# Attention's turns one unit later, late modulation sums one request later, in a one-core diffusion layer

## The chip, the core and the metric

The kernel runs on one core of one Trainium2 chip. What is measured is the device time of one execution in microseconds (us), lower is better. Each row of a profile comes from one execution that was recorded by the hardware profiler; its times are microseconds from the start of the span unless marked ns. The engines are TensorE (PE, with its weight loads as PEld), VectorE (DVE), ScalarE (ACT), GpSimd (POOL) and SyncE (SP, which here only issues DMAs).

## What is computed

One layer over 256 latent tokens and 256 context tokens, width 2048, all float32. Cut to its steps:

```
mod = silu(c) @ w_mod + b_mod                  # sa, ca, ga, sm, cm, gm: six vectors of 2048
h   = rmsnorm(x) * (1 + ca) + sa               # the same for the context tokens, with c_ctx
q, k, v, pool_in, gates = h @ w_in             # context gives k and v only
p   = softmax(q k^T / 8) per head half;  a = p0 - lam * p1;  heads = a @ v     # 8 heads
y_a = (rmsnorm(heads) * 0.8) @ w_a_up;  y_b = multiscale_pool(pool_in) @ w_b_up
x   = x + ga * ((g_a * y_a + g_b * y_b) @ w_o)     # g = sigmoid(gates)
x   = x + gm * (relu(modulate(x, sm, cm) @ w_ff1)^2 @ w_ff2)      # w_ff1: 2048 x 8192
```

`sa` and `ca` are needed at once. `ga`, `cm`, `sm` and `gm` are needed only from the product with `w_o` on; the kernel calls them late modulation.

## The kernel before, in words

**Weights.** All weights stream from HBM once, as chunks of 128 x 1024 floats (512 KB) in the order of a list `stream`. `load_next` issues one chunk's DMA on SP into one of five buffers `raw`, then splits it into two float32r parts: ACT casts `whi` (L195 before), DVE subtracts `wlo` (L196). A chunk's product takes three matmuls for each pair of slices (hi*hi, hi*lo, lo*hi). `whi` and `wlo` have three buffers each, so the split runs two chunks ahead of the matmuls. `wchunk` hands out the next chunk and calls `tick`.

**Late modulation.** `late_gen` is a generator with one step for each 128 x 1024 chunk of `w_ga`, `w_cm`, `w_sm`, `w_gm` (32 chunks each, two halves of 16). `load_next` adds a stage's rate to a credit and takes one step per whole credit: 1.0 for the first value group and the second query group, 1.5 for the second key and value groups, 0.75 in the pooling, 0.42 in the gates, 0.25 in the product with `w_o` (0 in its last group) and after. A step issues the chunk's DMA into the same five `raw` buffers and adds the chunk to an accumulator `macc` on DVE (L533). After 16 steps a half is split (`ah`, `al`) and summed over partitions by two matmuls with ones (`late_sum`).

**Deferred work.** `later(n, fn)` puts a function on a list; each `wchunk` ticks the list and runs what is due, so that `n` counts chunks. `flush` runs the whole list. Turning the normed queries and keys (`qkT`), the norm of a pair of heads (`osum`), the pooling's difference and the turning of the gated mixture (`mixT`) are put there.

**Attention** runs beside the bulk products. `run(bulk, side, EVERY)` advances the generator `attention` once for every 4.4 tokens' worth of bulk chunks. A unit is one head and one block of 128 queries: `scores` does two score matmuls (`sc`), then DVE takes the maxima (`mx`), ACT exponentiates (`e`), DVE combines the two halves into `e` (L602). `a_transpose` turns `e` on PE (`aTp`), `av` multiplies with the values (`ob`).

**The end of the product with `w_o`.** For its last group, g = 3, DVE and ACT instructions are held in program order (`ordered`): the residual, its squares, the rsqrt (`rsq`), then `flush()`, then the shift `yt` by `sm` (`shifted(0)`), whose turned result (`h2T`, `hidden2(0)`) the first MLP product waits for. Before it, a loop steps `late_gen` until `gm` has begun:

```
        if g == 3:
            while "gm" not in mods:
                next(late[0])
        ordered[0] = g == 3
```

**The order of instructions** on each engine is fixed when the program is built: a scheduler lists them by its own forecast of when each will be ready, except where `pin` (`keep_in_program_order`) holds an instruction in the order of the code. At run time every engine takes its list strictly in order.

Of the kernel before, what the change touches and what calls it, by code (L numbers as in the profile page):

```python
# [48 lines left out]
def layer(ctx: ExitStack, tc, a, out):  # L49
# [20 lines left out]
        return psum.tile([P, 512], F32, tag="ps", name=name)  # L70

    def work(name, shape=None, dt=F32):
        return pool.tile(shape or [P, 512], dt, tag="w2", name=name, bufs=7)

    def s16(name, shape, dt=F32):
        return pool.tile(shape, dt, tag="s16", name=name, bufs=7)
# [9 lines left out]

    late = [None]
    credit = [0.0]

    waiting = []  # L90

# [83 lines left out]
    def load_next():  # L175
        key, rate = stream[len(loaded)]
        src = a[key[0]]
        for i in key[1:]:
            src = src[i]
        if key[0] in ("cT", "x"):  # L180
            dst = cT[:, 4 * key[1]:4 * key[1] + 4, :] if key[0] == "cT" else x1_tile()[:, key[1], key[2] * 512:key[2] * 512 + 512]
            nc.sync.dma_start(dst, src)
            loaded.append((key, None, None))
            return
        n = src.shape[-1]
        raw = raw_chunk(src, n)
        if key[:2] in (("w_k", 0), ("w_q", 0)) and key[2] < 7:
            if not first:
                first.append(s16("first", [P, 4, 1024], F32R))
            i = 0 if key[0] == "w_k" else 2  # L190
            hi, lo = first[0][:, i, :], first[0][:, i + 1, :]
        else:
            hi = pool.tile([P, n], F32R, tag="whi", name="whi", bufs=3)
            lo = pool.tile([P, n], F32R, tag="wlo", name="wlo", bufs=3)
        act.copy(hi, raw)  # L195
        vec.tensor_sub(lo, raw, hi.bitcast(F32))  # L196
        loaded.append((key, hi, lo))
        credit[0] += rate
        while credit[0] >= 1.0:
            credit[0] -= 1.0  # L200
            if late[0] is not None:
                next(late[0], None)
# [309 lines left out]

    ga_bc = s8("ga_bc", [P, D])
    mods = {}

    def late_gen():
        for name in ("ga", "cm", "sm", "gm"):
            if name == "ga":
                dst = ga_bc
            elif name == "gm":  # L520
                mods["gm"] = s8("gm_bc", [P, D])
                dst = mods["gm"]
            else:
                if "sb" not in mods:
                    mods["sb"] = s16("sb", [P, 2, D])
                dst = mods["sb"][:, 0 if name == "cm" else 1, :]
            for half in range(2):
                acc = pool.tile([P, 1024], F32, tag="macc", name="macc", bufs=2)
                gp.memset(acc, 0.0)
                nc.gpsimd.dma_start(acc[0:1, :], a["b_" + name][half])  # L530
                for k in range(KT):
                    raw = raw_chunk(a["w_" + name][half, k])
                    vec.scalar_tensor_tensor(acc, raw, sil[:, 0, k:k + 1], acc, ALU.mult, ALU.add)  # L533
                    yield
                for q in range(2):
                    ah, al = work("ah", dt=F32R), work("al", dt=F32R)
                    split(ah, al, acc[:, q * 512:q * 512 + 512])
                    later(4 + q, partial(late_sum, name, ah, al, 2 * half + q,
                                         dst[:, half * 1024 + q * 512:half * 1024 + q * 512 + 512]))

    def late_sum(name, ah, al, i, o):

        ps = bank("late")
        pin(pe.matmul(ps, ones, ah, start=True, stop=False))
        pe.matmul(ps, ones, al, start=False, stop=True)
        if name == "cm":
            wr = work("nmw")
            nc.gpsimd.dma_start(wr, a["nmw"][i])
            vec.scalar_tensor_tensor(o, ps, 1.0, wr, ALU.add, ALU.mult)
        else:  # L550
            act.copy(o, ps)
# [14 lines left out]
    def k_group(g):  # L566
        bs = [bank(f"k{g}_{t}") for t in range(4)]
        yield from xstat(("w_k", g), bs, tokens(4))
        for t in range(4):
            qk_evac(bs[t], t, g, kT, 2, 2 + t)  # L570

    def q_group(g):
        bs = [bank(f"q{g}_{t}") for t in range(2)]
        for _ in xstat(("w_q", g), bs, tokens(2)):
            yield 0
        for t in range(2):
            qk_evac(bs[t], t, g, qT, 0, 3 + t)

    oT = pairtile("oT")
    heads = [0]  # L580
# [32 lines left out]
    def av(h):  # L613
# [7 lines left out]
        if h % 2 == 1:  # L621
# [14 lines left out]
                split(oT[:, 0, h - 1:h + 1, :], oT[:, 1, h - 1:h + 1, :], o2)  # L636
                heads[0] += 2

            later(3, norm)

    def attention(h0, h1):
        units = [(h, qt) for h in range(h0, h1) for qt in range(2)]
        prev = None
        for u in units + [None]:
            while u and turned[u[0] // 4] < 6 or prev and prev[0][1] == 1 and values[0] < prev[0][0]:
                yield
            cur = scores(*u) if u else None
            if prev is not None:
                (h, qt), at = prev
                a_transpose(h, qt, at)  # L650
                if qt == 1 and h > h0:
                    av(h - 1)
            if u is None:
                yield
                av(h1 - 1)
            prev = (u, cur)
            yield


    ybh = [None]  # L660
# [2 lines left out]
    def pooling():  # L663
# [3 lines left out]
        for g, w in enumerate(WINDOWS):  # L667
# [12 lines left out]
            for i in range(2):  # L680
# [8 lines left out]
                    src, oth = oth, src  # L689
                    step *= 2  # L690
                sums.append(src[:, s0:s0 + T])
            later(2, partial(pool_diff, g, w, ps, sums))
            if g > 0:
                pool_out(g - 1)

# [82 lines left out]

    run(v_group(0), iter(()), 1)
    run(chain(q_group(1), k_group(1), v_group(1), pooling(), gates()), attention(0, 8), EVERY)  # L780
    flush()
    tc.keep_in_program_order(act.preload_act_table_set("natural_log_exp_and_others"))


# [253 lines left out]
```

## Time and profile before

| what | before |
|---|---|
| median of 3 runs | 1548.26 us (1546.31 to 1548.51) |
| the profiled execution | 1548.65 us, of it 1546.8 us span |
| granted TensorE clock, mean | 0.989 of 2.4 GHz |
| busy share of the span: PE, DVE, ACT, POOL | 96%, 68%, 49%, 8% |
| moved by DMA | 347.83 MB, mean 225 GB/s |

The span is the time from the first instruction to the last. The difference of 1.85 us lies around it. PE is called busy while a matmul is in flight, also when it runs at half clock, so the busy share hides the half-clock stretches; the granted clock of a stretch tells them.

### The profile page before, as it was taken

What the parts mean: (1) busy time and instruction counts of PE and PEld (TensorE: products, weight loads), DVE (VectorE), ACT (ScalarE), POOL (GpSimd) and SP (SyncE); (2) the same over time, 40 slices, a digit from 0 to 9 for tenths busy, and PEclk for the clock granted to TensorE, in tenths of its full rate; (3) what the DMA queues carried; (4) which work ended last, traced back from release to release, by engine and by line L of the source; (5) the groups of instructions that cost most, each with busy time, mean ns of one, the idle gap of its engine ahead of it and who ended that gap; (6) DMA issues with size and microseconds to landing.
All of it is one profiled execution on the core that took longest, in us unless ns stands there. A gap on an engine that the chain in (4) does not pass through costs nothing.

```text
span 1546.8 us, 19707 instructions
## 1 busy us (share of the span) xinstructions
PE 1489.0 (96%) x7304; PEld 1236.5 (80%) x7304; DVE 1057.8 (68%) x1291; ACT 755.4 (49%) x1005; POOL 124.6 (8%) x124
## 2 busy tenths in 40 slices
PE   6999998899989999999998999999999999999998
PEld 4777776667778887887888988888888888888886
DVE  6998968677777676676677665666666555555575
ACT  7777533456544443443444554544445354444532
POOL 2000101010150000000000110000000000000170
PEclk9999999999999999999999999999999999999999
DMA  9888667543558877889675677777777666666563
GB/s 342 308 296 309 214 209 266 177 137 103 164 178 282 273 252 240 270 276 319 222 223 167 204 259 239 237 231 244 223 250 222 187 192 189 194 187 194 182 197 138
DMA packets 97440, 347.83 MB, mean 225 GB/s; under 512 B 11072, under 2 KB 11712, under 8 KB 97344
## 3 DMA queue, kind: packets, MB, share of 16 engines
q1 hardware_dynamic: 96624, 345.17, 69.1%
q8 instruction: 57, 0.93, 0.3%
q0 software_dynamic: 576, 1.08, 0.2%
q10 hardware_dynamic: 144, 0.33, 0.1%
q14 instruction: 39, 0.32, 0.1%
HBM read 344.44 MB, written 2.10 MB: 224 GB/s over the span
## 4 chain that ended last, share of the span: by engine, by line
PE 78%; DMA 9%; DVE 8%; issue 2%; ACT 2%; POOL 1%; DVEq 0%; ACTq 0%; POOLq 0%; SPq 0%
PE f L887 13%; PE f L387 8%; PE f L386 8%; PE f L389 7%; PE f L890 7%; PE pg L389 3%; PE pg L387 3%; PE pg L386 3%; DVE wlo L196 3%; DMA raw<-in_w_sm_dram 3%; DMA raw<-in_w_ga_dram 2%; DMA raw<-in_w_cm_dram 2%; PE mod L322 2%; PE wo L387 2%; PE wo L386 2%
## 5 line engine op out<-in xcount | busy, mean ns | idle before, releaser
L195 ACT CAST whi<-raw 128x1024 fp32r<-128x1024 f32 x501 | 523.4, 1047 | 581.4 <-PE f L387 177.0
L196 DVE TENSOR_TENSOR wlo<-raw,whi 128x1024 fp32r<-128x1024 f32 x501 | 614.6, 1239 | 260.4 <-ACT whi L195 249.6
L533 DVE SCALAR_TENSOR_TENSOR macc<-raw,sil,macc 128x1024 f32<-128x1024 f32 x128 | 166.4, 1300 | 146.2 <-DMA raw<-in_w_sm_dram 63.0
L887 PE MATMUL f<-h,whi 128*128 128x512 f32 x896 | 224.2, 392 | 0.0
L387 PE MATMUL f<-whi,act 128*128 128x512 f32 x512 | 199.3, 389 | 0.0
L386 PE MATMUL f<-whi,act 128*128 128x512 f32 x512 | 199.3, 389 | 0.0
L887 PEld LDWEIGHTS f<-h,whi 128*128 128x128 f32 x896 | 161.5, 189 | 29.1
L389 PE MATMUL f<-wlo,act 128*128 128x512 f32 x512 | 136.8, 389 | 0.0
L890 PEld LDWEIGHTS f<-h,wlo 128*128 128x128 f32 x896 | 122.2, 190 | 8.7
L890 PE MATMUL f<-h,wlo 128*128 128x256 f32 x896 | 124.9, 282 | 0.0
L389 PEld LDWEIGHTS f<-wlo,act 128*128 128x128 f32 x512 | 96.1, 188 | 20.0
L386 PEld LDWEIGHTS f<-whi,act 128*128 128x128 f32 x512 | 96.1, 188 | 19.8
L387 PEld LDWEIGHTS f<-whi,act 128*128 128x128 f32 x512 | 96.1, 188 | 19.8
L386 PE MATMUL pg<-whi,hL 128*128 128x512 f32 x256 | 100.9, 394 | 0.0
L387 PE MATMUL pg<-whi,hL 128*128 128x512 f32 x256 | 100.6, 393 | 0.0
L389 PE MATMUL pg<-wlo,hL 128*128 128x512 f32 x256 | 69.9, 395 | 7.7 <-DVE wlo L196 7.7
L898 POOL TENSOR_TENSOR rsq<-relu 128x512 f32<-128x512 f32 x28 | 29.2, 1042 | 546.1 <-ACT relu L897 536.0
L389 PEld LDWEIGHTS pg<-wlo,hL 128*128 128x128 f32 x256 | 48.3, 190 | 19.4 <-DVE wlo L196 9.6
L387 PEld LDWEIGHTS pg<-whi,hL 128*128 128x128 f32 x256 | 48.6, 190 | 10.2
L386 PEld LDWEIGHTS pg<-whi,hL 128*128 128x128 f32 x256 | 48.6, 190 | 10.2
L386 PE MATMUL wo<-whi,mix 128*128 128x512 f32 x128 | 50.5, 394 | 0.0
L387 PE MATMUL wo<-whi,mix 128*128 128x512 f32 x128 | 50.3, 393 | 0.0
(282 smaller groups left out, 2223.5 us busy)
## 6 DMA issues: line engine op xcount, KB each, us to landing
raw<-in_w_ff_dram SPq DMA_DIRECT2D x240, 512.0 KB, 4.1
raw<-in_w_m_dram SPq DMA_DIRECT2D x64, 512.0 KB, 5.1
raw<-in_w_ga_dram SPq DMA_DIRECT2D x32, 512.0 KB, 4.4
raw<-in_w_cm_dram SPq DMA_DIRECT2D x32, 512.0 KB, 4.3
raw<-in_w_gb_in_dram SPq DMA_DIRECT2D x32, 512.0 KB, 4.9
raw<-in_w_ga_in_dram SPq DMA_DIRECT2D x32, 512.0 KB, 4.6
raw<-in_w_sm_dram SPq DMA_DIRECT2D x32, 512.0 KB, 4.6
raw<-in_w_o_dram SPq DMA_DIRECT2D x32, 512.0 KB, 4.2
```

The lines of the kernel that those rows point to most:

```text
L195: act.copy(hi, raw)
L196: vec.tensor_sub(lo, raw, hi.bitcast(F32))
L322: pe.matmul(ps, cv[:, k, :], part[:, kk * 512:kk * 512 + 512], start=(k == 0 and part is hi), stop=(k == 15 and part is lo))
L386: pe.matmul(banks[t], tok(h, k, 0, tt), wt, start=k == 0, stop=False)
L387: pe.matmul(banks[t], tok(h, k, 1, tt), wt, start=False, stop=False)
L389: pe.matmul(banks[t], tok(h, k, 0, tt), wt, start=False, stop=k == 2 * nk - 1)
L533: vec.scalar_tensor_tensor(acc, raw, sil[:, 0, k:k + 1], acc, ALU.mult, ALU.add)
L887: pe.matmul(ps, hi[:, kk * P:kk * P + P], both(h2, k), start=k == 0, stop=False)
L890: pe.matmul(ps[:, T:2 * T], lo[:, kk * P:kk * P + P], act_slice(h2, k, 0), start=False, stop=k == KT - 1)
L898: gp.tensor_mul(sq, r, r)
```

## The change

It does five things. Attention keeps two units in flight: a unit's probabilities are turned after the scores of the second unit behind it. Turns of queries and keys, the pooling's difference and the heads' norm are due one or two chunks later. A late modulation chunk is added to `macc` by a function on the list, one tick (rate 1 or more) or two ticks (rate below 1) after its request, in program order on DVE; the accumulator has one buffer instead of two, and each half of 16 begins with an empty step. The `nmw` rows that `cm` is multiplied with are loaded at the half's ninth chunk, not in `late_sum`. The work buffers go from 7 to 9, and the `flush()` between the gates and the product with `w_o` is gone. The amount of arithmetic and of loaded bytes stays the same.

```diff
@@ -70,7 +70,7 @@
         return psum.tile([P, 512], F32, tag="ps", name=name)
 
     def work(name, shape=None, dt=F32):
-        return pool.tile(shape or [P, 512], dt, tag="w2", name=name, bufs=7)
+        return pool.tile(shape or [P, 512], dt, tag="w2", name=name, bufs=9)
 
     def s16(name, shape, dt=F32):
         return pool.tile(shape, dt, tag="s16", name=name, bufs=7)
@@ -86,6 +86,7 @@
 
     late = [None]
     credit = [0.0]
+    credit_rate = [0.0]
 
     waiting = []
 
@@ -196,6 +197,7 @@
         vec.tensor_sub(lo, raw, hi.bitcast(F32))
         loaded.append((key, hi, lo))
         credit[0] += rate
+        credit_rate[0] = rate
         while credit[0] >= 1.0:
             credit[0] -= 1.0
             if late[0] is not None:
@@ -512,6 +514,7 @@
 
     ga_bc = s8("ga_bc", [P, D])
     mods = {}
+    parts = []
 
     def late_gen():
         for name in ("ga", "cm", "sm", "gm"):
@@ -525,27 +528,45 @@
                     mods["sb"] = s16("sb", [P, 2, D])
                 dst = mods["sb"][:, 0 if name == "cm" else 1, :]
             for half in range(2):
-                acc = pool.tile([P, 1024], F32, tag="macc", name="macc", bufs=2)
+                yield
+                for part in parts:
+                    if part in waiting:
+                        waiting.remove(part)
+                        part[1]()
+                acc = pool.tile([P, 1024], F32, tag="macc", name="macc", bufs=1)
                 gp.memset(acc, 0.0)
                 nc.gpsimd.dma_start(acc[0:1, :], a["b_" + name][half])
+                norm_w = []
                 for k in range(KT):
                     raw = raw_chunk(a["w_" + name][half, k])
-                    vec.scalar_tensor_tensor(acc, raw, sil[:, 0, k:k + 1], acc, ALU.mult, ALU.add)
+                    if name == "cm" and k == 8:
+                        for q in range(2):
+                            norm_w.append(work("nmw"))
+                            nc.gpsimd.dma_start(norm_w[q], a["nmw"][2 * half + q])
+                    later(2 if credit_rate[0] < 1 else 1, partial(late_part, acc, raw, k))
+                    parts.append(waiting[-1])
+                    if k == KT - 1:
+                        o = dst[:, half * 1024:half * 1024 + 1024]
+                        later(2 if credit_rate[0] < 1 else 1, partial(late_split, acc, norm_w, o))
+                        parts.append(waiting[-1])
                     yield
-                for q in range(2):
-                    ah, al = work("ah", dt=F32R), work("al", dt=F32R)
-                    split(ah, al, acc[:, q * 512:q * 512 + 512])
-                    later(4 + q, partial(late_sum, name, ah, al, 2 * half + q,
-                                         dst[:, half * 1024 + q * 512:half * 1024 + q * 512 + 512]))
-
-    def late_sum(name, ah, al, i, o):
+
+    def late_part(acc, raw, k):
+
+        pin(vec.scalar_tensor_tensor(acc, raw, sil[:, 0, k:k + 1], acc, ALU.mult, ALU.add))
+
+    def late_split(acc, norm_w, o):
+        for q in range(2):
+            ah, al = work("ah", dt=F32R), work("al", dt=F32R)
+            split(ah, al, acc[:, q * 512:q * 512 + 512])
+            later(4 + q, partial(late_sum, ah, al, norm_w[q] if norm_w else None, o[:, q * 512:q * 512 + 512]))
+
+    def late_sum(ah, al, wr, o):
 
         ps = bank("late")
         pin(pe.matmul(ps, ones, ah, start=True, stop=False))
         pe.matmul(ps, ones, al, start=False, stop=True)
-        if name == "cm":
-            wr = work("nmw")
-            nc.gpsimd.dma_start(wr, a["nmw"][i])
+        if wr is not None:
             vec.scalar_tensor_tensor(o, ps, 1.0, wr, ALU.add, ALU.mult)
         else:
             act.copy(o, ps)
@@ -567,14 +588,14 @@
         bs = [bank(f"k{g}_{t}") for t in range(4)]
         yield from xstat(("w_k", g), bs, tokens(4))
         for t in range(4):
-            qk_evac(bs[t], t, g, kT, 2, 2 + t)
+            qk_evac(bs[t], t, g, kT, 2, 3 + t)
 
     def q_group(g):
         bs = [bank(f"q{g}_{t}") for t in range(2)]
         for _ in xstat(("w_q", g), bs, tokens(2)):
             yield 0
         for t in range(2):
-            qk_evac(bs[t], t, g, qT, 0, 3 + t)
+            qk_evac(bs[t], t, g, qT, 0, 4 + t)
 
     oT = pairtile("oT")
     heads = [0]
@@ -636,25 +657,24 @@
                 split(oT[:, 0, h - 1:h + 1, :], oT[:, 1, h - 1:h + 1, :], o2)
                 heads[0] += 2
 
-            later(3, norm)
+            later(5, norm)
 
     def attention(h0, h1):
         units = [(h, qt) for h in range(h0, h1) for qt in range(2)]
-        prev = None
-        for u in units + [None]:
-            while u and turned[u[0] // 4] < 6 or prev and prev[0][1] == 1 and values[0] < prev[0][0]:
+        behind = []
+        for u in units + [None, None]:
+            while u and turned[u[0] // 4] < 6 or len(behind) == 2 and behind[0][1] == 1 and values[0] < behind[0][0]:
                 yield
-            cur = scores(*u) if u else None
-            if prev is not None:
-                (h, qt), at = prev
+            if u:
+                behind.append((*u, scores(*u)))
+            if len(behind) > 2 or not u:
+                h, qt, at = behind.pop(0)
                 a_transpose(h, qt, at)
                 if qt == 1 and h > h0:
                     av(h - 1)
-            if u is None:
-                yield
-                av(h1 - 1)
-            prev = (u, cur)
             yield
+        av(h1 - 1)
+        yield
 
 
     ybh = [None]
@@ -689,7 +709,7 @@
                     src, oth = oth, src
                     step *= 2
                 sums.append(src[:, s0:s0 + T])
-            later(2, partial(pool_diff, g, w, ps, sums))
+            later(3, partial(pool_diff, g, w, ps, sums))
             if g > 0:
                 pool_out(g - 1)
 
@@ -778,7 +798,6 @@
 
     run(v_group(0), iter(()), 1)
     run(chain(q_group(1), k_group(1), v_group(1), pooling(), gates()), attention(0, 8), EVERY)
-    flush()
     tc.keep_in_program_order(act.preload_act_table_set("natural_log_exp_and_others"))
 
 
```

Three places show how this moves instructions. Numbers behind a tile's name rise with the order of the code.

On PE, in the second key group, between products of that group: `sc` are a unit's two score matmuls, `aTp` the turning of a unit's `e`. Before:

```order
L590 MATMUL sc_2289<-kT_1444,qT_1443 128x512
L590 MATMUL sc_2292<-kT_1444,qT_1443 128x512
L610 MATMUL aTp_2306<-prm_61,e_2232 128x128 x4
...
L590 MATMUL sc_2347<-kT_1444,qT_1443 128x512
L590 MATMUL sc_2350<-kT_1444,qT_1443 128x512
L610 MATMUL aTp_2363<-prm_61,e_2296 128x128 x4
```

After:

```order
L611 MATMUL sc_2334<-kT_1444,qT_1443 128x512
L611 MATMUL sc_2337<-kT_1444,qT_1443 128x512
L631 MATMUL aTp_2351<-prm_61,e_2216 128x128 x4
...
L611 MATMUL sc_2395<-kT_1444,qT_1443 128x512
L611 MATMUL sc_2398<-kT_1444,qT_1443 128x512
L631 MATMUL aTp_2411<-prm_61,e_2280 128x128 x4
```

`e_2296` of before belongs to the scores 2289 and 2292 and is turned behind the next unit's scores, with one chunk of 24 matmuls (left out) between. `e_2216` of after belongs to scores 2209 and 2212; the scores 2273, 2276 and 2334, 2337 and two chunks of 24 matmuls stand between it and its turning.

On DVE, in the gates, while `w_sm` is summed. `raw_` numbers are the order in which SP asks for the chunks; `macc` adds a late chunk, `wlo` splits a weight chunk. Before:

```order
L196 TENSOR_TENSOR wlo_4851<-raw_4848,whi_4850 128x1024
L533 SCALAR_TENSOR_TENSOR macc_4739<-raw_4893,sil_82,macc_4739 128x1024
L196 TENSOR_TENSOR wlo_4872<-raw_4869,whi_4871 128x1024
L196 TENSOR_TENSOR wlo_4890<-raw_4887,whi_4889 128x1024
L533 SCALAR_TENSOR_TENSOR macc_4739<-raw_4950,sil_82,macc_4739 128x1024
L196 TENSOR_TENSOR wlo_4911<-raw_4908,whi_4910 128x1024
```

After:

```order
L197 TENSOR_TENSOR wlo_5061<-raw_5058,whi_5060 128x1024
L556 SCALAR_TENSOR_TENSOR macc_4969<-raw_5044,sil_82,macc_4969 128x1024
L197 TENSOR_TENSOR wlo_5080<-raw_5077,whi_5079 128x1024
L197 TENSOR_TENSOR wlo_5100<-raw_5097,whi_5099 128x1024
L221 TENSOR_TENSOR mix0_3959<-mixT_5103,mix0_3959 128x512
L221 TENSOR_TENSOR mix0_3959<-mixT_5110,mix0_3959 128x512
L556 SCALAR_TENSOR_TENSOR macc_4969<-raw_5083,sil_82,macc_4969 128x1024
```

Before, `raw_4893` is added ahead of the splits of 4869 and 4887, which were asked for earlier. After, `raw_5044` is added behind the split of 5058, which was asked for later.

On DVE, from the rsqrt at the end of the product with `w_o` to the first MLP product; `rq_y` is the rsqrt, `yt` by L65 are the first shifts (`shifted(0)`), `al` splits a finished `macc`. Before:

```order
L65 SCALAR_TENSOR_TENSOR rq_y<-rq_t,rq_y 128x2
L65 SCALAR_TENSOR_TENSOR yt<-yt,rq_y,sb 128x256 x2
L822 SCALAR_TENSOR_TENSOR yt<-yt,rq_y,sb 128x256 x3
L65 TENSOR_TENSOR h_0_6766<-h2T,h_0_6766 128x512
L65 SCALAR_TENSOR_TENSOR yt<-yt,rq_y,sb 128x256 x2
```

After, from the row behind `rq_y` on:

```order
L65 SCALAR_TENSOR_TENSOR macc<-raw,sil,macc 128x1024
L841 SCALAR_TENSOR_TENSOR yt<-yt,rq_y,sb 128x256
L65 SCALAR_TENSOR_TENSOR macc<-raw,sil,macc 128x1024
L841 SCALAR_TENSOR_TENSOR yt<-yt,rq_y,sb 128x256
L65 SCALAR_TENSOR_TENSOR macc<-raw,sil,macc 128x1024
L841 SCALAR_TENSOR_TENSOR yt<-yt,rq_y,sb 128x256
L65 SCALAR_TENSOR_TENSOR macc<-raw,sil,macc 128x1024
L841 SCALAR_TENSOR_TENSOR yt<-yt,rq_y,sb 128x256
L65 SCALAR_TENSOR_TENSOR macc<-raw,sil,macc 128x1024 x2
L65 TENSOR_TENSOR al<-macc,ah 128x512 x2
L65 SCALAR_TENSOR_TENSOR yt<-yt,rq_y,sb 128x256 x2
L841 SCALAR_TENSOR_TENSOR yt<-yt,rq_y,sb 128x256 x5
```

Six sums, four other shifts and two splits now stand between the rsqrt and the first shift, and five other shifts instead of three behind it. The empty steps make the generator need 103 steps until `gm` begins instead of 97, while the stages' credits up to there still give 98; the loop above makes up the rest. On SP the last six `w_sm` chunks stand together behind the first chunk of the MLP, and on PE the four `late` matmuls of that half stand ahead of `h2T`, in both kernels.

## Rows read from the trace of the kernel before

**Rows 1.** The page: the chain that ended last, by engine, shares of the span.

```profile
PE 78%; DMA 9%; DVE 8%; issue 2%; ACT 2%; POOL 1%; DVEq 0%; ACTq 0%; POOLq 0%; SPq 0%
```

**Rows 2.** Stretches: busy PE, PEld, DVE, ACT, POOL (x count), PE clock, DMA share, GB/s.

```profile
205.00:233.00 28.00, 28.00 (x125) 23.17 (x125) 16.97 (x14) 11.55 (x14) 0.00 (x0) 1.00 0.70 231
362.00:452.00 90.00, 83.72 (x557) 73.70 (x556) 66.33 (x105) 52.59 (x94) 23.54 (x38) 0.96 0.53 164
...
900.00:950.00 50.00, 50.00 (x253) 42.62 (x252) 30.79 (x31) 26.04 (x34) 3.13 (x3) 1.00 0.76 249
```

**Rows 3.** Waits of PE: us in total, times, longest us.

```profile
PE pg L389 <- DVE wlo L196: 7.7, 4, 4.3
PE aTp L610 <- DVE e L602: 7.0, 6, 2.6
PE qkT L423 <- POOL qm L416: 6.8, 5, 3.6
...
PE h2T L829 <- DVE yt L65: 3.3, 1, 3.3
PE mixT L762 <- DVE sgm L752: 3.0, 2, 2.9
PE osum L630 <- POOL osq L626: 2.7, 1, 2.7
...
PE v L386 <- ACT e L596: 1.5, 1, 1.5
PE qkT L423 <- ACT aT L611: 1.0, 1, 1.0
```

**Rows 4.** Stretches from the end of a PE wait: columns as in rows 2.

```profile
417.30:421.30 4.00, 3.98 (x13) 3.26 (x14) 3.57 (x7) 2.29 (x6) 0.37 (x1) 0.57 0.67 200
...
463.60:470.00 6.40, 6.33 (x17) 5.00 (x18) 5.69 (x8) 2.37 (x3) 0.00 (x0) 0.58 0.74 217
...
825.70:831.20 5.50, 4.75 (x24) 4.33 (x25) 5.50 (x11) 2.48 (x3) 0.00 (x0) 0.69 0.07 7
```

**Rows 5.** PE in time, one unit of attention: start, duration, idle before and what ended it.

```profile
280.35 1.13 PE L590 MATMUL sc<-kT,qT 64*128 64x512 f32 x4
...
291.42 0.66 PE L610 MATMUL aTp<-prm,e 128*128 128x128 f32 x4 [1.63 <-DVE e L602]
```

**Rows 6.** DVE in time, the same unit.

```profile
288.14 1.29 DVE L533 SCALAR_TENSOR_TENSOR macc<-raw,sil,macc 128x1024 f32<-128x1024 f32 x1 [1.50 <-DMA raw<-in_w_ga_dram]
...
290.61 0.75 DVE L602 SCALAR_TENSOR_TENSOR e<-e,rs 128x512 f32<-128x512 f32 x1 [0.92 <-ACT e L601]
```

**Rows 7.** DVE in time, ahead of PE's longest wait of rows 3.

```profile
460.11 0.69 DVE L549 SCALAR_TENSOR_TENSOR sb<-late,nmw 128x512 f32<-128x512 f32 x1 [3.54 <-DMA nmw<-in_nmw_dram]
```

**Rows 8.** Who waited for whom, DVE on DMA: us, times, longest us.

```profile
DVE macc L533 <- DMA raw<-in_w_sm_dram: 63.0, 28, 4.1
```

**Rows 9.** DVE in time, around the end of the product with `w_o`.

```profile
806.68 1.29 DVE L219 TENSOR_TENSOR al<-macc,ah 128x512 fp32r<-128x512 f32 x2
...
810.63 1.28 DVE L533 SCALAR_TENSOR_TENSOR macc<-raw,sil,macc 128x1024 f32<-128x1024 f32 x1 [1.19 <-DMA raw<-in_w_gm_dram]
...
816.33 1.23 DVE L196 TENSOR_TENSOR wlo<-raw,whi 128x1024 fp32r<-128x1024 f32 x1 [1.50 <-ACT whi L195]
...
825.03 0.16 DVE L65 SCALAR_TENSOR_TENSOR rq_y<-rq_t,rq_y 128x2 f32<-128x2 f32 x1
825.23 0.88 DVE L65 SCALAR_TENSOR_TENSOR yt<-yt,rq_y,sb 128x256 f32<-128x256 f32 x2
```

**Rows 10.** ACT and PE in time, the same place.

```profile
805.99 1.12 ACT L218 CAST ah<-macc 128x512 fp32r<-128x512 f32 x2
...
825.77 0.83 PE L829 MATMUL h2T<-prm,yt 128*128 128x128 f32 x4 [3.28 <-DVE yt L65]
```

**Rows 11.** The page's DMA issues: count, KB each, median us to landing.

```profile
raw<-in_w_sm_dram SPq DMA_DIRECT2D x32, 512.0 KB, 4.6
```

**Rows 12.** Line 530, the accumulator's bias: us from issue to landing.

```profile
DMA to landing us min/median/max: 2.8/3.8/5.3
```

## The prediction

> **What bounds the kernel now.** I read the chain of work that ended last first: PE has 78% of it, so the end moves by what PE's list gains or loses [rows 1]. The stretches say where: from 900 us on PE is busy without a break at full clock, and nothing done there to another engine shows; from 362 to 452 us it is busy 83.7 of 90 us at a clock of 0.96 [rows 2]. DVE is busy 66.3 of those 90 us, so it isn't full, it is late. Then PE's waits. Those that the change can touch are the waits for the weight's lower part `wlo` (7.7 us in 4, the longest 4.3), for a unit's `e` (7.0 in 6), for the turns of queries and keys (6.8 behind POOL, 1.0 behind ACT), for the gated mixture (3.0), for the heads' squares (2.7) and for a bank of the second value group (1.5): 29.7 us [rows 3]. The 3.3 us for `yt`, at the end of the product with `w_o`, I keep apart.
>
> A wait costs more than itself. In the 4.0 us behind the wait at 417.3 the granted clock is 0.57, that is, part of it at 1.2 GHz instead of 2.4; (1 - 0.57) * 4.0 = 1.7 us of PE's work is lost. Behind the longest wait it is (1 - 0.58) * 6.4 = 2.7 us [rows 4]. The stretches behind the waits that end at 249.8, 443.9 and 731.5 us look like the first and lose 1.7 each. Together 4 * 1.7 + 2.7 = 9.5 us.
>
> **The change part by part.** Nothing is computed less, so each term is a wait with the slow stretch behind it, or a new wait.
>
> *Two units behind.* In the unit shown the second score matmul is done at 280.35 + 1.13 = 281.5, `e` at 290.61 + 0.75 = 291.4: 9.9 us [rows 5, 6]. In between PE had one chunk of 24 matmuls and the next scores; at 28.00/125 = 0.224 us for a matmul [rows 2] the chunk is 5.4 us. After, two chunks and two pairs of scores stand there, 2 * 5.4 + 2 * 1.1 = 13.0 us, over 9.9. Of the 9.9 us, 1.5 was one `macc` ahead in DVE's list that waited for its chunk [rows 6]; that goes too. I take the whole 7.0, and 1.7 behind 417.3: **8.7**.
>
> *Turns.* The longest wait for a turn is 3.6 [rows 3]; one chunk more, 5.4 us in that group, covers it, and the 1.0 behind ACT in the same way. With 1.7 behind 249.8: **6.3**. The other four waits for POOL (6.8 - 3.6 = 3.2) are mostly turns of the first groups, which get no longer lead; only DVE's list ahead of them is lighter by two sums of 1.28. I take half, **1.6**.
>
> *Norm of the heads.* The norm is due two chunks later, each at least 12 * 0.224 = 2.7 us of PE, so 5.4 us against a wait of 2.7: 2.7 + 1.7 = **4.4**.
>
> *`nmw`.* The 4.3 us wait for `wlo` is a queue on DVE: at 460.1 it had stood 3.54 us at the product with `nmw`, whose DMA had only just been asked for, and `wlo` stood behind it [rows 7]. After, `nmw` is asked for seven sums earlier: 4.3 + 2.7 = **7.0**.
>
> *Late sums in the order of their requests.* Before, DVE adds a chunk that was asked for last while two chunks asked for earlier still wait to be split; 28 such sums waited 63 us for `w_sm` alone [rows 8]. After, the request has the landing time of at least one chunk behind it. The other three waits for `wlo`, 7.7 - 4.3 = **3.4**, go.
>
> *No flush ahead of the product with `w_o`.* The mixture's last turn stands four chunks into that product instead of ahead of it, and the product needs it only at its seventh chunk: 3.0 + 1.7 = **4.7**. The bank wait of 1.5 may return elsewhere, since as many banks are in use as before; half, **0.8**.
>
> Gains together: 8.7 + 6.3 + 1.6 + 4.4 + 7.0 + 3.4 + 4.7 + 0.8 = 36.9 us.
>
> *The price: the empty steps.* Eight halves now begin with an empty step, so the generator is five steps short when `gm` must have begun. The loop asks for the last `w_sm` chunks in a row, and their sums run in `flush()`. By the order they stand on DVE behind the rsqrt and ahead of the first `yt`, for which PE waits. Before, `yt` starts 0.20 us behind the start of `rq_y` and `h2T` 0.54 after that [rows 9, 10]. After come six sums (6 * 1.28), four shifts (4 * 0.44), the first half's cast on ACT (0.56) and the two splits (1.29): 7.7 + 1.8 + 0.6 + 1.3 = 11.4 us [rows 9, 10]. Two more shifts stand ahead of the split of `h2T`: 0.9. The wait grows from 3.3 to about 15 us; the 4.3 us wait was followed by a loss of 2.7, the present one by (1 - 0.69) * 5.5 = 1.7 [rows 4], so 1.0 more. Sum **13.3**. Hidden is the loading: the last split of that product runs at 816.3, so four of the six chunks can be asked for 8 us ahead of the rsqrt. The fifth and sixth have to wait for the first and second sum; landing takes 4.6 [rows 11], and the fifth sum is due 4 * 1.28 + 4 * 0.44 = 6.9 us behind the rsqrt, 5.6 behind the first sum. If both land late instead, another 2 * 4.6 come on top; if the shifts cost nothing and the casts hide, it is 7.7 + 1.3 + 0.9. Bounds 9.9 and 22.5.
>
> *New waits, not shown by this trace.* With one accumulator a half's bias can land only after the last half's split. Where `w_ga` ends, one `wlo` stands between the split and the next half's first sum; a bias takes 3.8 us to land (2.8 to 5.3 [rows 12]), so DVE stands some 3 us, with two chunks split ahead for PE. The Trainium skill, "DMA: Bandwidth & Descriptors", section "Anatomy of one DMA", puts a transfer's fixed part at about 2.0 us and adds the bytes over 436 GB/s. By that the 4 KB bias would land in 2.0 us, and the trace's least is 2.8, so the trace doesn't agree; the sum stays the same by either, since two chunks cover both. A chunk that is added later holds its `raw` buffer longer, and weights share the five. In the second query group each 2.7 us chunk brings a second one, and there PE was busy 28.00 of 28 us with the DMA engines at 0.70 [rows 2]. From below both cost nothing; from above as much as all waits for `wlo` cost now, 7.7. I take **4**, between the two, for what a list in new order trips over.
>
> Sum: 1548.65 - 36.9 + 13.3 + 4 = 1529.05 us against the profiled execution, which lies 0.4 above the median of the runs shown. I say **1529**.
>
> **Rivals.** *The price eats the gain (slower).* One mechanism: at the end of the product with `w_o` the `w_sm` chunks find no free buffer and land one by one, each asked for when the one before is summed: 6 * (4.6 + 1.28) = 35.3 instead of 7.7 + 1.8, a price of 13.3 + 25.8 = 39.1. Then 1548.65 - 36.9 + 39.1 + 4 = 1555. It decides from a price of 33 on. Against it: five buffers are free of `w_o` by 817.6, and only one is taken by the MLP [rows 9].
>
> *DVE stays late.* The longer leads only move the waits: `e`, turns and heads' squares (8.7 + 6.3 + 4.4 = 19.4) come back by half, with new waits at 8: 1529 + 9.7 + 4 = 1543. For it: DVE was busy 66 of 90 us, and the same work will stand in a shorter stretch. Against: those waits were one late instruction each, not a full engine.
>
> *The buffers, not the order.* The Trainium skill, "Perfetto Trace Analysis", section "Optimization Strategy", says that the same gap repeating on the engine that should be full can mean too few SBUF or PSUM buffers. Here that would be a mechanism of its own: `e` or the turns wait for banks, and a longer lead holds more of them, so 19.4 us don't come: 1548. The rows name `e` on DVE and `qm` on POOL as what ended those waits, a bank only for 1.5 us [rows 3].
>
> *It doesn't do what it says for the late sums.* Their chunks are held longer, so weights are asked for later and `wlo` waits as before: 10.4 of gain less (7.0 + 3.4), 1539.
>
> **How the numbers follow.** The forecast has 0.60, DVE late 0.18, late sums without effect 0.08, buffers 0.06, the eaten gain 0.08. The likeliest case's own range is 1520 to 1537, by the price's bounds and new waits from 0 to 8. The range that leaves out no more than 2 in 10 is 1517 to 1545: below it lie new waits of 0 with the 1.6 and 0.8 doubled and a price of 10, above it the eaten gain and the buffers. A measurement of this kernel tells 0.2% (3 us) from no change. Faster by that: forecast, late sums without effect and most of DVE late, 0.84; within: buffers and a rest of DVE late, 0.07; slower: 0.09.
>
> **What would show it.** In the trace after, PE waits less than 2 us in all for `e`, no wait at the last `mixT`, and no wait of DVE for `nmw`; DVE's waits at `macc` for a chunk fall from 63 us for `w_sm` to a few. Ahead of `h2T` PE stands some 15 us with six sums on DVE in it; if it stands under 10 or over 22, my price is wrong. If the stretch from 205 to 480 us isn't some 20 us shorter, DVE was late for another reason than the order. A prediction too high would come from waits ahead of 205 us that go as well; too low, from weights that land late because late chunks hold their buffers.

## The result and the profile after

| | before | after |
|---|---|---|
| median of four runs each, on one chip | 1547.28 us (1545.41 to 1548.51) | 1535.44 us (1532.70 to 1537.14) |
| the profiled execution, its span | 1548.65, 1546.8 | 1537.14, 1535.0 |

The ratio is 0.9926, with a 95% interval of 0.9910 to 0.9943: 11.8 us faster, where I had forecast about 20. PE's share of the chain that ended last [rows 1] went up:

```profile
PE 86%; DVE 7%; ACT 3%; DMA 2%; issue 2%; POOL 0%; DVEq 0%; ACTq 0%; POOLq 0%; SPq 0%
```

PE's waits in the changed kernel (us in total, times, longest us) answer to [rows 3]:

```profile
PE late L567 <- ACT ah L65: 13.2, 1, 13.2
PE pd L224 <- ACT dh L220: 9.7, 2, 5.2
...
PE v L388 <- ACT e L617: 3.1, 1, 3.1
```

Gone from that list are `aTp`, `qkT`, `osum`, `mixT` and `pg` for `wlo`. The first row is the forecast price. The second is new: the pooling's product `pd` waits for `dh`, ACT's cast of the difference `d` that DVE computes. The third was 1.5 before: a bank of the second value group that an exponential frees.

To see where time went I cut the span at PE's first matmul of the first value group, the pooling, the gates, the product with `w_o` and the MLP. Columns as in [rows 2]; before, then after:

```profile
154.30:371.40 217.10, 203.52 (x891) 153.16 (x890) 165.45 (x266) 102.86 (x186) 18.12 (x14) 0.99 0.59 189
371.40:449.20 77.80, 71.52 (x501) 64.36 (x500) 57.78 (x93) 44.55 (x79) 19.26 (x32) 0.96 0.54 165
449.20:733.30 284.10, 273.12 (x1207) 224.25 (x1205) 194.39 (x191) 122.14 (x137) 11.86 (x16) 0.99 0.80 267
733.30:827.30 94.00, 90.04 (x395) 73.82 (x393) 64.20 (x74) 42.03 (x57) 1.45 (x2) 0.99 0.67 209
```

```profile
155.10:356.20 201.10, 197.26 (x871) 150.99 (x870) 155.76 (x254) 97.66 (x177) 19.33 (x13) 0.99 0.58 186
356.20:435.80 79.60, 69.92 (x494) 63.12 (x493) 60.04 (x95) 44.72 (x82) 16.22 (x30) 0.94 0.58 181
435.80:710.30 274.50, 274.50 (x1223) 227.48 (x1223) 196.61 (x190) 127.84 (x145) 15.86 (x19) 0.99 0.81 268
710.30:815.50 105.20, 91.32 (x401) 74.67 (x399) 76.55 (x90) 41.71 (x57) 1.45 (x2) 0.94 0.71 223
```

Values, queries and keys take 16.0 us less, the gates 9.6 less, the pooling 1.8 **more**, the product with `w_o` 11.2 more. The pooling is where the forecast broke. DVE in the changed kernel, ahead of the first wait at `pd`:

```profile
387.92 0.69 DVE L235 SCALAR_TENSOR_TENSOR rq_t<-rq_y 128x512 f32<-128x512 f32 x1
...
394.70 0.68 DVE L221 TENSOR_TENSOR oT<-osb,oT 128x512 fp32r<-128x512 f32 x1
395.31 0.15 DVE L722 TENSOR_TENSOR zb<-zb,prm 128x1 f32<-128x1 f32 x1
...
396.01 0.42 DVE L726 SCALAR_TENSOR_TENSOR d<-zb,pin 128x256 f32<-128x256 f32 x1
```

And PE at the same place (start, duration, idle before and its releaser):

```profile
390.07 1.89 PE L640 MATMUL ob<-aT,v 128*128 128x256 f32 x8
...
397.14 0.58 PE L224 MATMUL pd<-dh,whi 128*128 128x256 f32 x1 [5.18 <-ACT dh L220]
```

From `rq_t` to `oT` DVE works through a norm of heads (with splits and maxima between); the difference `d` stands behind it, and PE, done at 392.0, stands 5.2 us until ACT has cast `d` into `dh`. At 435.45 the same happens again, with 4.5.

### The profile page after: what moved, and what is told of

Read it like the earlier page. It is cut to its first block, busy times and chain, and to the rows that moved or that the text cites. A ratio compares the mean times of both kernels' runs of the same rounds, so it can differ in the third digit from the quotient of the medians.

```text
span 1535.0 us, 19705 instructions
## 1 busy us (share of the span) xinstructions
PE 1485.2 (97%) x7304; PEld 1238.3 (81%) x7304; DVE 1063.6 (69%) x1291; ACT 756.2 (49%) x1005; POOL 127.0 (8%) x124
## 4 chain that ended last, share of the span: by engine, by line
PE 86%; DVE 7%; ACT 3%; DMA 2%; issue 2%; POOL 0%; DVEq 0%; ACTq 0%; POOLq 0%; SPq 0%
PE f L906 13%; PE f L389 8%; PE f L388 8%; PE f L391 8%; PE f L909 7%; PE pg L388 4%; PE pg L389 4%; PE pg L391 4%; DVE wlo L197 2%; PE wo L388 2%; PE pyy L388 2%; PE wo L391 2%; PE pyy L389 2%; PE wo L389 2%; PE pyy L391 2%; PE mod L324 2%
## 5 line engine op out<-in xcount | busy, mean ns | idle before, releaser
L197 DVE TENSOR_TENSOR wlo<-raw,whi 128x1024 fp32r<-128x1024 f32 x501 | 618.1, 1238 | 371.4 <-ACT whi L196 362.7
L556 DVE SCALAR_TENSOR_TENSOR macc<-raw,sil,macc 128x1024 f32<-128x1024 f32 x122 | 160.1, 1313 | 3.6 <-DMA macc<-in_b_cm_dram 3.5
```

Of the source, the lines that this page charges most:

```text
L556: pin(vec.scalar_tensor_tensor(acc, raw, sil[:, 0, k:k + 1], acc, ALU.mult, ALU.add))
```

## The experiments

Stretches in us, as cut above (setup ahead of them; the MLP is 718.2 to 720.6 in all), of each kernel's profiled execution, and the median of its timed runs. The kernels were measured in four groups, each with the kernel before beside it; its medians there were 1547.3, 1547.7, 1547.7 and 1549.1. So the ratios compare best. The intervals of norm at 6, sums at request, `nmw` late and flush overlap that of the changed kernel, so what these four say rests on their waits and stretches. And a profiled execution is only one of a kernel's: that of the changed kernel, 1537.14 us, is the slowest of its four, and what the others gain on it lies between 2 us less and 5 us more than by the medians.

| kernel | setup | q, k, v | pooling | gates | w_o | median | ratio to before, 95% |
|---|---|---|---|---|---|---|---|
| changed | 155.1 | 201.1 | 79.6 | 274.5 | 105.2 | 1535.44 | 0.9910 to 0.9943 |
| difference at 2 | 154.8 | 201.3 | 74.4 | 271.8 | 105.3 | 1529.21 | 0.9854 to 0.9891 |
| norm at 3 | 155.7 | 203.2 | 73.3 | 270.8 | 105.3 | 1526.97 | 0.9840 to 0.9879 |
| norm at 6 | 154.2 | 201.5 | 72.5 | 277.3 | 105.2 | 1533.85 | 0.9886 to 0.9932 |
| one unit behind | 154.7 | 203.1 | 75.1 | 270.4 | 105.3 | 1532.53 | 0.9876 to 0.9907 |
| turns as before | 155.7 | 207.0 | 70.0 | 271.0 | 105.3 | 1528.24 | 0.9846 to 0.9884 |
| rate 0.5 in w_o | 156.3 | 201.7 | 79.3 | 274.2 | 95.0 | 1527.36 | 0.9838 to 0.9875 |
| sums at request | 154.2 | 197.9 | 83.1 | 272.9 | 101.8 | 1534.81 | 0.9890 to 0.9931 |
| `nmw` late | 158.1 | 201.2 | 75.9 | 273.9 | 105.3 | 1532.74 | 0.9881 to 0.9921 |
| flush | 154.1 | 200.8 | 79.2 | 277.1 | 106.0 | 1538.86 | 0.9921 to 0.9964 |
| norm 6, rate 0.5 | 155.3 | 203.1 | 74.0 | 275.8 | 95.0 | 1524.72 | 0.9824 to 0.9871 |
| norm 3, rate 0.5 | 155.0 | 202.9 | 73.3 | 270.9 | 95.0 | 1518.57 | 0.9788 to 0.9820 |
| the same, sums at request | 156.9 | 201.3 | 75.4 | 273.1 | 95.0 | 1524.02 | 0.9816 to 0.9853 |

**The difference back at two chunks.**

```diff
-            later(3, partial(pool_diff, g, w, ps, sums))
+            later(2, partial(pool_diff, g, w, ps, sums))
```

> The changed kernel with the pooling's difference due two chunks behind its request again instead of three; nothing else. Theory A (the difference's own later turn makes PE wait, since the product that needs it did not move): the two waits of PE at pd for dh, 9.7 us in the changed kernel, fall under 2 us, the half-speed stretches at 396 and 434 us (6.8 us each, some 2.7 lost in each) go, and the time falls by 10 to 15 us, to 1520-1526. Theory B (the heads' norm, now due five chunks late, comes due in the same chunk and stands on DVE ahead of the difference): over 5 us of the pd waits stay and the time falls by less than 5 us.

No wait at `pd` is left, and the time falls by 6.2 us: theory A's mechanism, but less than its 10 to 15 us. DVE in this kernel, around the same place:

```profile
382.68 0.41 DVE L726 SCALAR_TENSOR_TENSOR d<-zb,pin 128x256 f32<-128x256 f32 x1
...
388.05 0.69 DVE L235 SCALAR_TENSOR_TENSOR rq_t<-rq_y 128x512 f32<-128x512 f32 x1
```

The difference is now 5 us ahead of the norm instead of behind it. Against the gain stands a new wait of PE (`pin` for `wlo`, 3.8 us in 3).

**The norm back at three, and on to six.**

```diff
-            later(5, norm)
+            later(3, norm)      # first kernel
+            later(6, norm)      # second kernel
```

> The changed kernel with the heads' norm due three chunks behind its request again instead of five; the difference stays at three. Theory B (the norm ahead of the difference on DVE is what delays it): the pd waits fall from 9.7 to under 3 us; a wait at osum for the heads' squares of 2 to 3 us may return; time lower by 6 to 12 us. Theory A: the pd waits stay above 7 us, the osum wait returns with some 1.7 us of clock, and the time is the same or up to 5 us higher.

> The changed kernel with the heads' norm due six chunks behind its request instead of five; the difference stays at three. Both bringing the difference forward and bringing the norm forward took the waits at pd away, so the theory now is that the two fall due in the same place of DVE's list, the norm first. Then moving the norm further back cures it too: pd waits under 2 us, no osum wait, time lower than the changed kernel's 1535.4 by 6 to 10 us (1525-1529). Rival (the norm is simply too late, and what holds it longer holds buffers): pd waits stay above 7 us or other waits of that size come, time 1534 or more.

Moved forward, the norm gives 8.5 us: 1.4 us of waits at `pd` are left and 3.4 at `osum` come back. So theory A alone is wrong: with the difference still at three, the waits go. DVE here:

```profile
383.18 0.68 DVE L235 SCALAR_TENSOR_TENSOR rq_t<-rq_y 128x512 f32<-128x512 f32 x1
...
388.82 0.42 DVE L726 SCALAR_TENSOR_TENSOR d<-zb,pin 128x256 f32<-128x256 f32 x1
```

Most of the norm still stands ahead of the difference, but it starts 4.7 us earlier, and `d` is done at 389.2, before PE asks for it at 392.7. What counts is when the norm lets the difference through, not only which of the two stands first. Moved back, the norm stands behind the difference, and the waits at `pd` go too (0.8 left), as the collision says, but others come:

```profile
PE pg L391 <- DVE wlo L197: 2.2, 1, 2.2
PE late L567 <- ACT e L617: 2.1, 2, 1.7
```

Its six runs spread from 1530.87 to 1537.24, so the median can hardly be told from the changed kernel's; the pooling is 7.1 us shorter, the gates 2.8 longer. The place was right, the size of the gain was not.

**Attention one unit behind, and the turns as before.** These undo two parts of the change whole.

```diff
# first kernel: attention() as in the kernel before (prev instead of behind)
# second kernel:
-            qk_evac(bs[t], t, g, kT, 2, 3 + t)
+            qk_evac(bs[t], t, g, kT, 2, 2 + t)
-            qk_evac(bs[t], t, g, qT, 0, 4 + t)
+            qk_evac(bs[t], t, g, qT, 0, 3 + t)
```

> The changed kernel with attention's probabilities turned one unit behind their scores again. Prediction's term: PE waits at aTp for e return with about 7.0 us and 1.7 us of clock, time higher by 7 to 10 us. Rival (the late sums' new order had already taken most of e's delay from DVE's list): the aTp waits return with less than 3 us and the time rises by less than 4 us.

> The changed kernel with the turns of the second groups' queries and keys due one chunk earlier again (keys 2 and later, queries 3 and later). Prediction's term: PE's waits at qkT for POOL's qm return with 3.6 us, 1.0 us behind ACT and a half-speed stretch worth 1.7 us: the stretch from the first value group to the pooling grows from 201.2 us by 5 to 7 us. Rival (two units behind had already moved what the turns waited for, and the turns only change places with other waits): that stretch grows by less than 2 us. The time moves with it, 1535.4 plus 5 to 7 or plus less than 2.

Both came out faster than the changed kernel, by 2.9 and 7.2 us, which neither side expected. One unit behind, PE waits for `e` again, about as priced:

```profile
PE aTp L631 <- DVE e L623: 7.6, 6, 2.4
```

3.6 of it up to the pooling. Queries, keys and values grow by 2.0 us only: the wait for a bank at `v` falls from 3.1 to 0.2. And the waits at `pd` fall from 9.7 to 0.7, and pooling and gates shrink by 8.6. With the old turns the first stretch grows by 5.9, as forecast (3.2 of it waits at `qkT` for POOL), and pooling and gates shrink by 13.1. DVE in the kernel with the old turns shows the first wait at `pd`:

```profile
392.19 0.69 DVE L221 TENSOR_TENSOR oT<-osb,oT 128x512 fp32r<-128x512 f32 x1
...
396.94 0.40 DVE L726 SCALAR_TENSOR_TENSOR d<-zb,pin 128x256 f32<-128x256 f32 x1
```

The norm stands ahead of the difference here too, and `d` is done at 397.3, against 396.4 in the changed kernel; but PE began the pooling at 362.7 instead of 356.2, so it waits 1.4 us there and not 5.2. DVE's list set the time of `d`; the 6 us that the turns won on PE only made PE come earlier to it. The second wait, 4.5 us, doesn't come at all, since the old turns move something else too. By the code the units of the second half of the heads start only when the second groups' queries and keys are turned. The score matmuls of the changed kernel and, below them, of the one with the old turns (first and last start):

```profile
L611 PE MATMUL sc<-kT,qT x64: 589/641/693, 248.3 to 407.7; 64*128 64x512 f32 x64
L611 PE MATMUL sc<-kT,qT x64: 589/641/693, 251.7 to 393.8; 64*128 64x512 f32 x64
```

The last scores come 51.5 us into the pooling in the changed kernel and 31.1 with the old turns. The norms come earlier with them, and the second `d` is done at 429.1, before PE starts its `pd` at 431.3; in the changed kernel it is done at 434.8. Neither kernel undoes its part with the norm at three, so the runs don't show what the two parts are worth without the collision.

**More late modulation in the product with `w_o`.**

```diff
-            plan("w_o", g, ch, rate=0.25 if g < 3 else 0.0)
+            plan("w_o", g, ch, rate=0.5 if g < 3 else 0.0)
```

> The changed kernel with 0.5 instead of 0.25 requests of the late modulation per chunk in the product with w_o, so that all its sums are done ahead of the end of that product. By the price of the prediction (13.3 us for six sums, their two splits and the shifts between rsqrt and first transpose): PE's wait of 13.2 us at late becomes one of some 3.3 us at h2T for yt, the half-speed stretch of 17.1 us shrinks to some 7, time lower by 10 to 14 us, 1521-1525. Rival (the sums only move their delay): the weights of w_o wait on DVE for the added sums, PE waits for wlo there by 5 us or more in all, and the time falls by less than 6 us.

8.1 us faster, where 10 to 14 were expected. The product with `w_o` takes 95.0 us instead of 105.2, no wait for `wlo` comes in it, and PE's wait there is

```profile
PE h2T L848 <- DVE yt L65: 4.2, 1, 4.2
```

So the six sums were the price, towards its lower bound of 9.9: the stretch gets 10.2 us back.

**Sums at their request; `nmw` late; the flush.**

```diff
# first kernel
-                    later(2 if credit_rate[0] < 1 else 1, partial(late_part, acc, raw, k))
-                    ...
+                    late_part(acc, raw, k)           # late_split in the same way
# second kernel: late_sum asks for nmw where it multiplies with it
# third kernel, ahead of the product with w_o
+    flush()
```

> The changed kernel with each late modulation chunk added, and each half split, at its request again; the earlier request of the norm weights, the empty steps and the single accumulator stay. Prediction's term: DVE waits at macc for chunks return with tens of us, and PE waits for wlo return with some 3.4 us and for e in part (up to 5 us): time higher than 1535.4 by 3 to 9 us. Rival of the prediction (late sums without effect on PE): DVE's waits return, but PE's waits for wlo and e grow by under 1.5 us and the time stays within 2 us. The six sums at the end of the product with w_o then wait for their chunks as well, which may add up to 10 us there.

> The changed kernel with the norm weights asked for only when their sum is multiplied, as before the change; the late sums stay behind their requests. Prediction's term: DVE stands some 3 us at the product with nmw again, wlo behind it is late by some 4 us for PE, with a half-speed stretch worth 2.7: the stretch from the first gate product to the product with w_o grows from 274.4 us by 5 to 8 us. Rival (the new order of DVE's list puts chunks of slack behind that product): DVE waits there, PE's wait for wlo grows by less than 1.5 us, and the stretch by less than 2 us.

> The changed kernel with all deferred work run ahead of the product with w_o again, late sums included. Prediction's term: PE's wait of some 3 us at mixT returns with a half-speed stretch worth 1.7 us, time higher by 4 to 6 us (1539-1541). Rival: the mixture's last turn is as late four chunks into the product, so that nothing was gained there: time within 2 us of 1535.4.

The first stays within 2 us of the changed kernel, as the rival has it, but both sides missed what DVE does: its waits for chunks do **not** return. Before, they were 63.0 + 36.5 + 34.0 + 12.2 = 145.7 us; here DVE waits on a DMA at `macc` once, for a bias:

```profile
DVE macc L554 <- DMA macc<-in_b_cm_dram: 1.2, 1, 1.2
```

So the delay by one or two chunks is not what removed them. What this kernel still shares with the changed one does: sums pinned in the order of the code, one accumulator, the empty steps. The runs don't tell these apart. Nor did DVE's standing go with these waits; most of it moved to the splits (113.1 us more there). Before, changed, sums at request:

```profile
DVE wlo L196 <- ACT whi L195: 249.6, 209, 5.2
DVE wlo L197 <- ACT whi L196: 362.7, 320, 5.3
DVE wlo L197 <- ACT whi L196: 351.0, 330, 5.1
```

In all, DVE is idle 489.0 us of the span before and 471.4 after. The price didn't rise as feared either: the product with `w_o` takes 3.4 us less. With `nmw` asked for late, the median is 2.7 us lower, not higher, but DVE stands again, as priced:

```profile
DVE sb L571 <- DMA nmw<-in_nmw_dram: 2.9, 2, 2.7
```

PE's waits for `wlo` behind it come to 1.1 us (one at `pyy`). The gates take 273.9 us, 0.6 less than in the changed kernel, but that one has the slow stretch behind its second wait at `pd` in them, and here this wait is 2.3 us with none behind it. Against the kernels that have none either (270.8 with norm at 3, 271.8 with the difference at 2) it is 2 to 3 us longer, between the rival's bound of 2 and the term's 5 to 8; that this is `nmw` alone is argued, since the difference or the norm moved in these two. The flush brings a wait of 1.7 us at `mixT` back and costs 3.4 us in the medians, 2.6 in the gates and 0.8 in the product with `w_o`; the term was 4.7.

**Two cures together.** Norm at six or three, each with the rate of 0.5; then the second of these with sums at their request.

> Two cures together: the heads' norm due six chunks behind its request, and 0.5 instead of 0.25 requests of the late modulation per chunk in the product with w_o. If the two costs are independent, the gains add: 6 to 10 us for the waits at pd and 8 us for the sums at the end of that product (1535.4 to 1527.4 when it was raised alone), so 1518-1521. If one hides behind the other it stays at 1525 or more. PE's waits left from 150 us on: about 3 us at the first matmul of the second value group for a bank, 4 us at h2T for yt, and less than 3 us of others.

> Two cures together again, with the norm due three chunks behind its request, which had measured 1526.97 alone, and 0.5 requests per chunk in the product with w_o. If the gains add: 1526.97 minus 8 to 10, that is 1517 to 1520. By stretch: first value group to pooling 203, pooling 73, gates 271, product with w_o 95 us, as each had it alone. If they don't: gates or pooling longer by over 3 us than alone, 1522 or more.

> The same as the one with norm at three chunks and 0.5 requests per chunk, with the late sums added at their request again. It tells what the new order of the late sums is worth where the waits at pd don't cover it. Prediction's term (3.4 us of waits for wlo, and 1.5 us of each late unit's e): slower than its pair by 3 to 6 us. Rival (without effect on PE, or worse, since sums that are held back meet other work on DVE): within 2 us of its pair, or up to 4 us faster, the gain between the first value group and the pooling, as that stretch was 197.9 us with sums at their request and 201.2 with sums behind it.

With norm at six it is 1524.72, above the 1518 to 1521 expected; but that norm alone had measured only 1.6, and 1.6 + 8.1 = 9.7 stands against 10.7. With norm at three the gains add as well: 8.5 + 8.1 = 16.6 by the kernels with one cure each, 16.9 measured. At 1518.57 us (0.9804 of before) it is the fastest of all. The last kernel is 5.5 us slower in the medians, so here the delay of the sums does pay. The profiled pair shows 2.1 + 2.2 in pooling and gates, -1.6 ahead of them, and 1.9 in the setup, whose code is the same. But no wait for `wlo` or `e` comes back, as the term had it: PE waits 5.9 us instead of 3.4 at `osum`, and 2.1 instead of 1.4 at `pd`.

## Why the prediction was right and where it failed

By stretch the forecast was 12.5 us of gain up to the pooling (3.8 of the two units, 7.9 of turns, 0.8), 24.4 in pooling and gates (there 0.56 + 2.59 of the waits for `e`, at 396.9 and 417.3, with the 1.7 behind), a price of 13.3 and new waits of 4. Measured were 16.0, 7.8 and 11.2. So the first stretch gave 3.5 us more and the price was 2.1 less than forecast, and both hid part of the 12.6 that pooling and gates fell short: that the total came so near is partly luck. Of the 16.0, undoing the two units and the turns returns 2.0 and 5.9; the other 8 no run here assigns to a part.

- **Two units behind (8.7).** The waits for `e` are gone, and undoing it brings 7.6 us back; right as a wait. But it holds banks longer (3.1 us at `v` instead of 1.5, where I had counted a gain of 0.8) and the norms fall later. With the norm at five it is worth nothing as an edit: without it the kernel is faster by 2.9.
- **Turns (6.3 and 1.6).** Undone they cost 5.9 us in their stretch; right. All waits behind POOL went, not half.
- **Norm (4.4).** Undone, 3.4 us of waits at `osum` return, but the waits at `pd` go. The step counted the wait that the norm's later turn removes, and not what the norm then stands in front of.
- **`nmw` (7.0).** The mechanism on DVE was right (2.9 us against 3), the worth of the edit was not: 2 to 3 us by the stretches, with 1.1 us of PE's waits for `wlo` where the term has 4.3.
- **Late sums (3.4).** DVE's waits at `macc` and PE's for `wlo` went as forecast, but not by the delay that I named, and DVE's standing mostly moved to its splits.
- **No flush (4.7).** 3.4 by the medians, and as much by gates and product with `w_o`.
- **The price (13.3).** Six sums, no DMA wait among them, 13.2 us of standing where I had said 15, 11.2 us more in the stretch. The mechanism was right, the sum 2 us too high. From the rsqrt to PE's first turning it is 0.74 us before [rows 9, 10] and 11.92 now:

```profile
801.88 0.16 DVE L65 SCALAR_TENSOR_TENSOR rq_y<-rq_t,rq_y 128x2 f32<-128x2 f32 x1
...
813.80 1.05 PE L848 MATMUL h2T<-prm,yt 128*128 128x128 f32 x4
```

That is 11.2 more, the sum's 11.4 for sums, shifts, cast and splits. The two terms on top, 0.9 for two shifts and 1.0 for the clock, don't show: PE is at half clock behind this wait as behind those at `pd`, but the first products of the MLP were slow in the kernel before too (first row below; then the changed kernel behind the two waits at `pd` and the one of 13.2), and the MLP takes 719.5 us in both.

```profile
827.30:831.20 3.90, 3.90 (x20) 3.90 (x21) 3.90 (x6) 1.82 (x2) 0.00 (x0) 0.56 0.09 9
397.10:403.10 6.00, 5.96 (x28) 5.96 (x29) 3.60 (x6) 3.74 (x10) 2.71 (x6) 0.50 0.41 133
435.40:440.70 5.30, 5.25 (x18) 4.64 (x19) 5.26 (x5) 3.40 (x8) 3.95 (x5) 0.50 0.47 155
811.60:819.50 7.90, 7.20 (x26) 5.90 (x27) 7.78 (x15) 4.14 (x6) 1.45 (x2) 0.50 0.41 147
```

- **New waits (4), the step that failed.** The text took 4 us "for what a list in new order trips over" and looked for it at bias loads and `raw` buffers. At a bias DVE does stand 3.5 us once, as the text said, and PE doesn't feel it. What cost time was the pooling's difference, which the change moved by a chunk while its consumer stayed, behind the heads' norm, which it moved by two. Both moves were named and neither was priced for this: 9.7 us of waits and 0.5 * (6.0 + 5.3) = 5.6 of clock, 15 us as an estimate. Taking the waits away returns 6.2 (difference at 2) or 8.5 us (norm at 3) in the medians, 7.9 and 10.0 in pooling and gates. That is less than 15, and other waits came (3.8 us at `pin`, 3.4 at `osum`); it is about the 7.8 by which the gain fell short (19.6 by the sum, 11.8 measured).
- **Rivals.** The eaten gain didn't happen. "DVE stays late" was nearest: its waits for `e`, turns and squares didn't come back, but DVE's list was the limit in the pooling all the same, and my own test said so (the first two stretches are 294.9 - 280.7 = 14.2 us shorter, not 20). The buffers: the one wait for a bank doubled to 3.1 us, and the waits at `pd` were ended by ACT's `dh`, data and no bank. The Trainium skill, "Perfetto Trace Analysis", section "Optimization Strategy", lets a gap that repeats point to too few buffers; the two like gaps at `pd` are no such case, since with the same buffers another place of the norm or of the difference removes them.

The time lies inside the likeliest case's own range, 1520 to 1537, near its upper end. Open: which of the pin, the single accumulator and the empty steps took DVE's 145.7 us of waits at `macc` away, and what the two more work buffers do, which no run here undoes.

## What to carry to other kernels

When several deferred steps get longer leads at once, price for each not only the wait that it leaves but what it then stands ahead of on the in-order engine, and check that a producer whose lead grows has a consumer that moved too. A gain on the bounding engine is kept only as long as the engine that feeds it is ahead: cut the span at the same instructions before and after, and look which stretch gives the gain back. Undo each part alone on the changed kernel; here two parts that were right by their own waits made the whole slower, for they moved the norms as well as their own step.

## What I had not expected of the hardware

Behind the waits of 5.2, 4.5 and 13.2 us the granted clock was 0.50 (1.2 GHz) for 6.0, 5.3 and 7.9 us; behind the waits of 2.6 and 4.3 us before it was 0.57 and 0.58 on average over 4.0 and 6.4 us [rows 4]. So the longest wait was followed by 0.50 * 7.9 = 4.0 us of lost work, as an estimate, where I had counted 2.7; the length of the stretches doesn't show the difference. And the setup, with the same code in all kernels, took from 154.1 to 158.1 us, so that a difference of 4 us between two profiled executions says nothing until it is found in a stretch that the edit touches.
